# State-space scan of a hybrid trunk: the samples' token parts four-fold from memory, and like products of the second mixer side by side

## The chip, the cores and the metric

The kernel runs on one core of a Trainium2 chip. The metric is the device time of one execution in microseconds (us). A profile is one execution that the hardware profiler recorded. Its engines are TensorE (PE, with the weight loads as PEld), VectorE (DVE), ScalarE (ACT), GpSimd (POOL) and SyncE (SP), which here issues every transfer.

## The reference, cut to what matters

Four layers run over 512 prompt tokens and 8 samples of 8 tokens, 576 columns in all: convolution and attention, a feed-forward layer, a Mamba-2 mixer, and another feed-forward layer. The change is in the Mamba-2 mixer. Its scan, with 32 heads in 4 groups, head width 64 and state size 128, for each chunk of tokens:

```
acum   = cumsum(dt * a)                      # per head, within a chunk
decay  = exp(where(causal, acum_l - acum_s, -inf))
cb     = C_l . B_s                           # per group
y_diag = (cb * decay * dt) @ x               # inside the chunk
states = B . (exp(acum_end - acum) * dt) . x # what a chunk adds to the state
h      = exp(acum_end) * h + states          # from chunk to chunk
y_off  = C . h_before * exp(acum)            # what earlier chunks carry in
y      = y_diag + y_off + d_skip * x
```

The prompt is four chunks of 128 tokens and starts from zero. Each of the 8 samples is one chunk of 8 tokens and starts from a state in memory (h0). Both final states are outputs (ssm_p and ssm_s).

## The kernel before

Activations lie with channels on partitions and the 576 tokens as columns. A weight matrix comes from memory in tiles of 128 by 1024 (wr), and ACT and DVE split it into a high and a low part (wh, wl). Each projection product is three products of 128 by 288 (L160, L161, L162, tile mm). This projection stream fills TensorE nearly everywhere.

In the second mixer, `ssd(g)` is a generator that does the scan of one group, g = 0 to 3. `run(main, side)` interleaves it with units of the projection stream: the input projection of the next group, the output projection of the group before. After that a scheduler puts each engine's instructions in its own order, by estimated durations and priorities. `keep_in_program_order(m)` pins a product right behind the one written before it. Every engine works through its order strictly in turn.

Temporary tiles come from a ring of equal slots: `S(...)` takes a slot, `free(...)` returns it, and the slot returned longest ago is given out next. Whoever writes into a slot waits for its last user, and that can be a transfer to memory. TensorE's result banks are divided likewise: three for the projection (mm), two for the scan's products (aux: transposes pt, state products pst, carried products py), two for the outputs (yp), and one shared by ysp and pyo.

One scan in the order of the code, by tile names:

- btok (L951): transposes of B for the prompt. r3 (L958): B and x of the samples, each token column repeated three times; L966 and L979 transpose these, and bp, b3, xf and x3 (L968 to L985) are the parts that `finish` multiplies. b3 and x3 hold three partial terms on 96 rows, 32 rows for each. dd3 (L923 to L928) holds the factors that belong to x3.
- pc (L994), cbm: C.B, masked.
- xdt (L1007, L1009): transposes of x in five chunks of tokens, times dt; chunk 4 is the samples'.
- xde, pst, hst (L1018 to L1026): the states from chunk to chunk; out_ssm_p (L1030) writes the last one.
- es (L1035 to L1041) for the samples. `decays(r)` for each of 8 heads: acb is loaded from the kernel's own memory acd (L1047), four Relus (L1051), exponential (L1052), mask (L1053). `carried(t)`: ea loaded (L1060), exponential, py (L1064), product (L1066). `outputs(t)`: yp (L1077), and the sums into xs.
- `load` brings h0 (L1092), `begin` makes pyo and scales h0 on POOL, `finish` adds pst (L1118, b3 times x3) to h0 and writes out_ssm_s (L1120). ysp (L1145, L1150) is the samples' output.

Of the kernel before, what the change touches and what calls it, by code (L numbers as in the profile page):

```python
# [8 lines left out]
F32 = mybir.dt.float32  # L9
# [5 lines left out]
P = 128  # L15
# [25 lines left out]
for _name, _w in (  # L41
    ("ident", 128), ("m32", 32), ("prot", 128), ("blk2", 2), ("amask", 256), ("smask", 2 * 192),
    ("tri", 128), ("tris", 64), ("bmat", 64), ("bsel", 8), ("selx", 256), ("selm", 128),
    ("sel3", 192), ("bsel3", 4),
):
    CV[_name] = _n
    _n += _w
# [3 lines left out]
class Builder:  # L51
    NSLOT = 48
    EXTRA = 11
# [750 lines left out]
    def mix1(self):  # L804
# [86 lines left out]
        da = self.Z("da", W, bufs=1)  # L891
        nc.vector.scalar_tensor_tensor(da.rearrange("p (c h) -> p c h", h=32), dt.rearrange("p (c h) -> p c h", h=32), -1.0,
                                       ea.unsqueeze(1).broadcast_to([P, 5, 32]), op0=MUL, op1=MUL)
        dab = self.Z("dab", 256, rows=64, bufs=1)
# [9 lines left out]
        nc.tensor.matmul(pb[:, 160:416], self.ones[0:64, :], dab, start=True, stop=True)  # L904
        ac, de = (self.Z(n_, W, bufs=1) for n_ in ("ac", "de"))
# [16 lines left out]

        dtde, dd3 = self.Z("dtde", 32, rows=64, bufs=1), self.Z("dd3", 64, rows=96, bufs=1)  # L923
        nc.vector.tensor_tensor(dtde, dt[0:64, 128:160], de[0:64, 128:160], op=MUL)
        pe = self.ps("pe")
        for bh in range(2):
            nc.tensor.matmul(pe[0:96, bh * 32:bh * 32 + 32], self.cv("sel3", bh * 96, 96, 64), dtde, start=True, stop=True)
        nc.vector.tensor_copy(dd3, pe[0:96, 0:64])  # L928
# [15 lines left out]
        def ssd(g):  # L944
# [10 lines left out]
            r3 = []  # L955
            for a in [bf] + xs:
                r3.append(self.S("r3", 192))
                nc.scalar.activation(r3[-1].rearrange("p (b r t) -> p b r t", r=3, t=32),  # L958
                                     a[:, NP:T].rearrange("p (b t) -> p b t", t=32).unsqueeze(2).broadcast_to([P, 2, 3, 32]),
                                     AF.Copy)  # L960
            rep3 = lambda i, bh: r3[i][:, bh * 96:bh * 96 + 96]
            pt = self.ps("pt")
            b3 = []
            for bh in range(2):
                o = pt[0:96, bh * P:(bh + 1) * P]
                nc.tensor.transpose(o, rep3(0, bh), self.ident)  # L966
                bp = self.S("bp", P, F32R, rows=96)
                nc.scalar.activation(bp, o, AF.Copy)  # L968
                nc.vector.tensor_tensor(bp[64:96, :], o[64:96, :], bp[64:96, :].bitcast(F32), op=SUB)
                b3.append(self.S("b3", NP, F32R, rows=96))  # L970
                nc.vector.tensor_tensor(b3[bh].rearrange("p (b n) -> p b n", n=P),
                                        bp.bitcast(F32).unsqueeze(1).broadcast_to([96, 4, P]),
                                        self.cv("bsel3", 0, 4, 96).unsqueeze(2).broadcast_to([96, 4, P]), op=MUL)
                self.free(bp)
            x3 = []
            for bh in range(2):
                pt = self.ps("pt")
                for t in range(4):
                    nc.tensor.transpose(pt[0:96, t * P:(t + 1) * P], rep3(1 + t, bh), self.ident)  # L979
                xf = self.S("xf", NP, rows=96)  # L980
                nc.vector.tensor_tensor(hp(xf), hp(pt[0:96, :]),
                                        dd3[:, bh * 32 + 8 * g:bh * 32 + 8 * g + 8].unsqueeze(2).broadcast_to([96, 8, 64]), op=MUL)
                x3.append(self.S("x3", NP, F32R, rows=96))
                nc.scalar.activation(x3[bh], xf, AF.Copy)
                nc.vector.tensor_tensor(x3[bh][32:64, :], xf[32:64, :], x3[bh][32:64, :].bitcast(F32), op=SUB)  # L985
                self.free(xf)
                yield
            self.free(r3)
# [13 lines left out]
            xdt = []  # L1002
            for c in range(5):
                n = P if c < 4 else 64
                pt = self.ps("pt")
                for t in range(4):
                    nc.tensor.transpose(pt[0:n, t * P:(t + 1) * P], xs[t][:, c * P:c * P + n], self.ident)  # L1007
                o = self.S("xdt", NP, rows=n)
                nc.vector.tensor_tensor(hp(o), hp(pt[0:n, :]), dt[0:n, hs(c)].unsqueeze(2).broadcast_to([n, 8, 64]), op=MUL)  # L1009
                xdt.append(o)  # L1010
                if c % 2:
                    yield
            yield

            H = []
            for c in range(4):
                xde = self.S("xde", NP)
                nc.vector.tensor_tensor(hp(xde), hp(xdt[c]), de[:, hs(c)].unsqueeze(2).broadcast_to([P, 8, 64]), op=MUL)  # L1018
                pst = self.ps("pst")
                nc.tensor.matmul(pst, btok[:, c * P:(c + 1) * P], xde, start=True, stop=True)  # L1020
                hn = self.S("hst", NP)
                if c == 0:
                    nc.scalar.activation(hn, pst, AF.Copy)
                else:
                    nc.vector.tensor_tensor(hp(hn), hp(H[-1]), cd[:, hs(c)].unsqueeze(2).broadcast_to([P, 8, 64]), op=MUL)
                    nc.vector.tensor_tensor(hn, hn, pst, op=ADD)  # L1026
                self.free(xde)
                H.append(hn)
                yield
            nc.sync.dma_start(d["ssm_p"][g], H[3])  # L1030
            self.free(H.pop(), btok)
            yield

# [10 lines left out]
            def decays(r):  # L1044

                acb = self.S("acb", NP)
                nc.sync.dma_start(acb, acd[8 * g + r, 0:NP].partition_broadcast(P))  # L1047
                for c in range(4):
                    cs = slice(c * P, (c + 1) * P)
                    o = c * 32 + 8 * g + r  # L1050
                    nc.scalar.activation(acb[:, cs], acb[:, cs], AF.Relu, bias=ac[:, o:o + 1], scale=-1.0)  # L1051
                self.last_exp = nc.scalar.activation(acb, acb, AF.Exp, scale=-1.0).ins  # L1052
                nc.vector.tensor_tensor(acb, acb, cbm[:, :NP], op=MUL)  # L1053
                return acb

            def carried(t):

                ea2 = self.S("ea2", NP - P)
                for hh in range(2):
                    nc.sync.dma_start(ea2[hh * 64:hh * 64 + 64, :], acd[8 * g + 2 * t + hh, P:NP].partition_broadcast(64))  # L1060
                nc.scalar.activation(ea2, ea2, AF.Exp)
                py = self.ps("py")
                for c in range(1, 4):
                    nc.tensor.matmul(py[:, (c - 1) * P:c * P], H[c - 1][:, t * P:(t + 1) * P], cf[:, c * P:(c + 1) * P],  # L1064
                                     start=True, stop=True)
                nc.vector.tensor_tensor(ea2, ea2, py[:, 0:NP - P], op=MUL)  # L1066
                return ea2
# [44 lines left out]
            def finish(bh, behind):  # L1112

                for b4 in range(4):
                    b = 4 * bh + b4
                    pst = self.ps("pst")
                    with self.tc.issue_after(behind):
                        nc.tensor.matmul(pst, b3[bh][:, b4 * P:(b4 + 1) * P], x3[bh], start=True, stop=True)  # L1118
                    nc.vector.tensor_tensor(h0[bh][b4], h0[bh][b4], pst, op=ADD)
                    nc.sync.dma_start(d["ssm_s"][b, g], h0[bh][b4])  # L1120
                    self.free(h0[bh][b4])
                    if b4 % 2:
                        yield
# [23 lines left out]
            for t in range(4):  # L1147
                o = ysp[:, t * 64:t * 64 + 64]
                for bh in range(2):
                    nc.tensor.matmul(o, yo[bh][:, t * P:(t + 1) * P], self.cv("selm", bh * 64, 64), start=False, stop=bh == 1,  # L1150
                                     skip_group_check=True)
                nc.vector.scalar_tensor_tensor(xs[t][:, NP:], xs[t][:, NP:], self.pv("dsk", 4 * g + t), o, op0=MUL, op1=ADD)
# [34 lines left out]
        def run(main, side):  # L1187

            n, k = 30, 0
# [74 lines left out]
def constants():  # L1264
# [24 lines left out]
    for bh in range(2):  # L1289
# [6 lines left out]
        put("sel3", (tok[:, None] == bh * 32 + np.tile(np.arange(32), 3)[None, :]).astype(f), bh * 96)  # L1296
# [114 lines left out]
```

## Time and profile before

| quantity | value |
|---|---|
| three runs | 1564.84, 1567.7 and 1568.19 us; median 1567.7 |
| profiled execution | 1567.04 us; span 1565.3 |
| granted TensorE clock, mean | 0.997 |
| scan of group 0, 1, 2, 3 (us of the span) | 699.3 to 766.8, 794.3 to 868.9, 913.7 to 987.0, 1031.8 to 1098.3 |
| TensorE busy there | 63.61 of 67.50, 72.11 of 74.60, 71.13 of 73.30, 64.57 of 66.50 |

How to read the profile's rows. A row of the waits says who waited, on which tile and line, for whom: total us, times, the longest. A row of a group of instructions has line, engine, operation, tile out<-in, shape and count, then busy us, mean ns of one, and the idle time just ahead with what ended it. A row of order of time has start, duration, engine, line, operation and count. A row of the stretches has the stretch, its length, busy us of an engine (number of instructions), clock, share of the transfers, GB/s. A row of the transfers has their count, KB each, and the median us from issue to landing. TensorE's instructions overlap, so a duration is longer than the distance from one start to the next.

### The profile page before, as it was taken

What the parts mean: (1) busy time and instruction counts of PE and PEld (TensorE: products, weight loads), DVE (VectorE), ACT (ScalarE), POOL (GpSimd) and SP (SyncE); (2) the same over time, 40 slices, a digit from 0 to 9 for tenths busy, and PEclk for the clock granted to TensorE, in tenths of its full rate; (3) what the DMA queues carried; (4) which work ended last, traced back from release to release, by engine and by line L of the source; (5) the groups of instructions that cost most, each with busy time, mean ns of one, the idle gap of its engine ahead of it and who ended that gap; (6) DMA issues with size and microseconds to landing.
All of it is one profiled execution on the core that took longest, in us unless ns stands there. A gap on an engine that the chain in (4) does not pass through costs nothing. (4 is left out here: it accounts for less than half of the span.)

```text
span 1565.3 us, 28515 instructions
## 1 busy us (share of the span) xinstructions
PE 1538.9 (98%) x11661; PEld 1471.1 (94%) x11661; DVE 1002.2 (64%) x1766; ACT 642.3 (41%) x1201; POOL 148.5 (9%) x365
## 2 busy tenths in 40 slices
PE   8999999999999999999999999999999999999999
PEld 7968799999999999997998998998999999999999
DVE  7858877563564464677796677676966643563552
ACT  6247553221222222475765655656542221221220
POOL 0026101000000000011202002002010000000000
PEclk9999999999999999999999999999999999999999
DMA  8504232222222222226345235235322222222232
GB/s 235 130 30 112 86 98 88 88 82 81 81 79 85 90 87 63 76 84 183 103 131 171 93 102 182 94 107 180 99 82 81 81 83 86 88 72 92 81 86 75
DMA packets 69361, 157.61 MB, mean 101 GB/s; under 512 B 19678, under 2 KB 24030, under 8 KB 69230
## 3 DMA queue, kind: packets, MB, share of 16 engines
q1 hardware_dynamic: 69230, 155.79, 32.5%
q8 instruction: 92, 1.51, 0.4%
q14 instruction: 39, 0.32, 0.1%
HBM read 140.55 MB, written 15.21 MB: 100 GB/s over the span
## 5 line engine op out<-in xcount | busy, mean ns | idle before, releaser
L160 PE MATMUL mm<-hh,wh 128*128 128x288 f32 (+1 forms) x2288 | 682.1, 299 | 7.3 <-ACT wh L150 6.9
L162 PE MATMUL mm<-hh,wl 128*128 128x288 f32 x2288 | 681.5, 298 | 1.0 <-DVE wl L151 1.0
L161 PE MATMUL mm<-hl,wh 128*128 128x288 f32 x2288 | 678.2, 297 | 0.0
L150 ACT ACTIVATE wh<-wr 128x1024 fp32r<-128x1024 f32 (+1 forms) x215 | 223.5, 1040 | 544.6 <-issue 270.7
L160 PEld LDWEIGHTS mm<-hh,wh 128*128 128x128 f32 (+1 forms) x2288 | 431.2, 189 | 12.1 <-ACT wh L150 7.2
L162 PEld LDWEIGHTS mm<-hh,wl 128*128 128x128 f32 x2288 | 430.6, 188 | 4.8 <-issue 2.0
L161 PEld LDWEIGHTS mm<-hl,wh 128*128 128x128 f32 x2288 | 432.0, 189 | 2.6 <-DVE hl L171 0.6
L151 DVE TENSOR_TENSOR wl<-wr,wh 128x1024 fp32r<-128x1024 f32 (+1 forms) x215 | 260.1, 1210 | 82.0 <-ACT wh L150 81.9
L161 PE MATMUL mm<-yl,wh 128*128 128x288 f32 x960 | 286.1, 298 | 0.2 <-DVE yl L171 0.2
L160 PE MATMUL mm<-yh,wh 128*128 128x288 f32 x960 | 285.3, 298 | 0.7 <-DVE x L259 0.7
L162 PE MATMUL mm<-yh,wl 128*128 128x288 f32 x960 | 283.3, 296 | 0.3 <-DVE wl L151 0.3
L160 PEld LDWEIGHTS mm<-yh,wh 128*128 128x128 f32 x960 | 180.4, 188 | 4.1 <-DVE x L259 1.8
L161 PEld LDWEIGHTS mm<-yl,wh 128*128 128x128 f32 x960 | 180.8, 188 | 2.7 <-issue 1.4
L162 PEld LDWEIGHTS mm<-yh,wl 128*128 128x128 f32 x960 | 180.4, 188 | 1.5 <-issue 0.9
L259 DVE TENSOR_TENSOR x<-x,mm 128x288 f32<-128x288 f32 x192 | 84.9, 450 | 144.2 <-PE mm L162 143.8
L304 DVE TENSOR_TENSOR gbuf<-mm,rs 128x224 f32<-128x224 f32 x44 | 17.2, 391 | 107.9 <-PE mm L162 107.9
L315 ACT ACTIVATE gsilu<-gconv,par 128x512 f32<-128x512 f32 x44 | 31.8, 723 | 115.7 <-DVE gconv L312 115.7
L312 DVE SCALAR_TENSOR_TENSOR gconv<-gbuf,par,gconv 128x592 f32<-128x592 f32 x88 | 73.1, 831 | 1.5
L325 DVE TENSOR_TENSOR gsilu<-mm,gsilu 128x288 f32<-128x288 f32 x88 | 40.0, 454 | 49.6 <-PE mm L162 49.6
L830 DVE SCALAR_TENSOR_TENSOR cconv<-cbuf,par,cconv 128x600 f32<-128x600 f32 x72 | 60.2, 840 | 11.6 <-ACT cconv L828 10.7
L1051 ACT ACTIVATE acb<-acb,ac 128x128 f32<-128x128 f32 x128 | 41.3, 390 | 46.7 <-DMA acb<-acd 29.3
L307 POOL COPY fpo<-gbuf 128x2 f32<-128x2 f32 x44 | 12.4, 283 | 473.2 <-DVE gbuf L304 473.2
(311 smaller groups left out, 1600.3 us busy)
## 6 DMA issues: line engine op xcount, KB each, us to landing
wr<-in_w_gate SPq DMA_DIRECT2D x44, 512.0 KB, 3.3
wr<-in_w_up SPq DMA_DIRECT2D x44, 512.0 KB, 3.3
wr<-in_w_in_o SPq DMA_DIRECT2D x40, 512.0 KB, 3.4
wr<-in_w_down SPq DMA_DIRECT2D x32, 448.0 KB, 3.3
wr<-in_w_down SPq DMA_DIRECT2D x16, 512.0 KB, 3.5
acb<-acd SPq DMA_DIRECT2D x32, 256.0 KB, 4.1
h<-in_h SPq DMA_DIRECT2D x32, 256.0 KB, 3.6
out_ssm_s<-h SPq DMA_DIRECT2D x32, 256.0 KB, 2.5
```

What stands on the lines that cost most here:

```text
L150: nc.scalar.activation(hi[:, :n], raw[:, :n], AF.Copy)
L151: nc.vector.tensor_tensor(lo[:, :n], raw[:, :n], hi[:, :n].bitcast(F32), op=SUB)
L160: nc.tensor.matmul(out, hi[:, ws], xh[:, sl], start=i == 0, stop=False)
L161: nc.tensor.matmul(out, hi[:, ws], xl[:, sl], start=False, stop=False)
L162: nc.tensor.matmul(out, lo[:, ws], xh[:, sl], start=False, stop=i == n - 1)
L259: nc.vector.tensor_tensor(self.x[m][:, sl], self.x[m][:, sl], p[:, :HB], op=ADD)
L304: nc.vector.tensor_tensor(g[:, 290:514], p[:, 0:224], rs[:, HB:NP], op=MUL)
L312: nc.vector.scalar_tensor_tensor(cv[:, :592], g[:, k:592 + k], w(k), cv[:, :592], op0=MUL, op1=ADD)
L315: nc.scalar.activation(sl[:, :NP], cv[:, :NP], AF.Silu, bias=b)
L325: nc.vector.tensor_tensor(sl[:, HALF[half]], p[:, :HB], sl[:, HALF[half]], op=MUL)
L830: nc.vector.scalar_tensor_tensor(cv[:, :600], g[:, k:600 + k], w(k), cv[:, :600], op0=MUL, op1=ADD)
L1051: nc.scalar.activation(acb[:, cs], acb[:, cs], AF.Relu, bias=ac[:, o:o + 1], scale=-1.0)
```

## The change

It takes the r3 copies, their transposes (L966, L979) and dd3 with its products out. In their place, B of the samples is transposed once (L949 of after) and written to a new place in the kernel's own memory, bx. The samples' x parts, already transposed as xdt chunk 4, are multiplied by de (x64) and written there too (L982). `four` reads each half back with every row block four times, onto 128 rows instead of 96 (bf4, xf4, L992), and b3 and x3 are made from these, behind the states in the code. Chunk 4 of xdt now comes first.

The state products come in pairs with the two halves side by side; `finish` makes its products in pairs; transposes, py and ysp products are pinned in a row. `carried(t + 1)` is called right behind the outputs of t. The masks of a group must run in head order. Two tiles (da, dab) move into the ring, and the ring has one more slot.

```
-    EXTRA = 11
+    EXTRA = 12
...
-            r3 = []
-            for a in [bf] + xs:
-                r3.append(self.S("r3", 192))
-                nc.scalar.activation(r3[-1]..., a[:, NP:T]... repeated 3 times, AF.Copy)
...
-                nc.tensor.transpose(o, rep3(0, bh), self.ident)
...
-                    nc.tensor.transpose(pt[0:96, t * P:(t + 1) * P], rep3(1 + t, bh), self.ident)
...
+            nc.tensor.transpose(pt[0:64, 0:P], bf[:, NP:T], self.ident)
+            bx = self.dp.tile([64, NP + P], F32, name=f"bx{g}")
+            b64 = self.S("b64", P, rows=64)
+            nc.scalar.activation(b64, pt[0:64, 0:P], AF.Copy)
+            nc.sync.dma_start(bx[:, NP:], b64)
...
-            for c in range(5):
+            for c in (4, 0, 1, 2, 3):
...
-                for t in range(4):
-                    nc.tensor.transpose(pt[0:n, t * P:(t + 1) * P], xs[t][:, c * P:c * P + n], self.ident)
+                for t in (3, 0, 1, 2):
+                    m = nc.tensor.transpose(pt[0:n, t * P:(t + 1) * P], xs[t][:, c * P:c * P + n], self.ident)
+                    if t < 3:
+                        self.tc.keep_in_program_order(m)
...
+                if c == 4:
+                    x64 = self.S("x64", NP, rows=64)
+                    nc.vector.tensor_tensor(hp(x64), hp(o), de[0:64, hs(4)]..., op=MUL)
+                    nc.sync.dma_start(bx[:, 0:NP], x64)
...
+            def four(name, bh, o, n):
+                t = self.S(name, n)
+                rows = bx[bh * 32:bh * 32 + 32, o:o + n]
+                nc.sync.dma_start(t, bass.AP(tensor=rows.tensor, offset=rows.offset, ap=[[0, 4], list(rows.ap[0]), [1, n]]))
+                return t
...
+            for c0 in (0, 2):
...
+                pst = [self.ps("pst") for _ in range(2)]
+                for c in (c0 + 1, c0):
+                    m = nc.tensor.matmul(pst[c - c0], btok[:, c * P:(c + 1) * P], xde[c - c0], start=True, stop=True)
+                self.tc.keep_in_program_order(m)
...
+            b3, x3 = [], []
+            raw = [(four("bf4", bh, NP, P), four("xf4", bh, 0, NP)) for bh in range(2)]
+            yield
+            for bh, (br, xf) in enumerate(raw):
+                bp = self.S("bp", P, F32R)
+                nc.scalar.activation(bp, br, AF.Copy)
...
+                nc.scalar.activation(x3[bh], xf, AF.Copy)
...
+                if r:
+                    self.tc.add_manual_dep(m.ins, self.last_mask.name, ..., reason="masks in turn")
...
-                ea2 = carried(t)
+                if t == 0:
+                    ea2 = carried(0, False)
...
+                if t < 3:
+                    ea2 = carried(t + 1)
...
-            n, k = 30, 0
+            n, k = 29, 0
```

SyncE's queue as the third scan begins, before (h is h0; ea, acb and es are the loads of decay factors):

```order
L141 DMA wr<-in_w_in_o 128x1024 x2
L1092 DMA h_10398<-in_h 128x512
L1092 DMA h_10400<-in_h 128x512
L1092 DMA h_10402<-in_h 128x512
L1060 DMA ea_10404<-acd 64x384 x2
L1047 DMA acb<-acd 128x512
L1035 DMA es<-acd 64x8x64
L1092 DMA h_10396<-in_h 128x512
```

and after, down to the first loads of decay factors (bx is the kernel's own memory, bf and xf the four-fold reads):

```order
L141 DMA wr<-in_w_in_o 128x1024 x2
L953 DMA bx_10125<-b_10126 64x128
L992 DMA bf_10329<-bx_10125 128x1x128
L992 DMA bf_10333<-bx_10125 128x1x128
L1037 DMA es<-acd 64x8x64
L982 DMA bx_10125<-x_10146 64x512
L992 DMA xf_10331<-bx_10125 128x1x512
L992 DMA xf_10335<-bx_10125 128x1x512
L1100 DMA h_10359<-in_h 128x512
L1100 DMA h_10363<-in_h 128x512
L1100 DMA h_10361<-in_h 128x512
L1066 DMA ea_10437<-acd 64x384 x2
```

Two writes and four reads have come in, all ahead of the h0, ea and acb loads.

ACT's order at the same place, before (x is x3, hst the first state out of its result bank):

```order
L958 ACTIVATE r_10158<-xs 128x192
L984 ACTIVATE x_10180<-xf 96x512
L150 ACTIVATE wh<-wr 128x1024
L984 ACTIVATE x_10190<-xf 96x512
L1061 ACT_TABLE_LOAD
L1061 ACTIVATE ea_10404<-ea_10404 128x384
L1051 ACTIVATE acb<-acb,ac 128x128 x4
L1052 ACTIVATE acb<-acb 128x512
L1023 ACTIVATE hst<-pst 128x512
```

and after:

```order
L1025 ACTIVATE bp<-bf_10329 128x128
L1025 ACTIVATE bp<-bf_10333 128x128
L150 ACTIVATE wh<-wr 128x1024
L1032 ACTIVATE x_10342<-xf_10331 128x512
L1009 ACTIVATE hst<-pst 128x512
L1032 ACTIVATE x_10350<-xf_10335 128x512
L1067 ACT_TABLE_LOAD
```

The first x3 copy, which needs the read from bx, now stands right ahead of the state's copy (L1009), and the second right behind it; before, both x3 copies had no transfer to wait for.

DVE's order after, at the same place (b is b3, x_10342 and x_10350 are x3, x_77 and x_78 are rows of the residual):

```order
L1011 TENSOR_TENSOR hst<-hst,cd 128x512
L1033 TENSOR_TENSOR x_10342<-xf_10331,x_10342 32x512
L1012 TENSOR_TENSOR hst<-hst,pst 128x512
L259 TENSOR_TENSOR x_78<-x_78,mm 128x288
L1011 TENSOR_TENSOR hst<-hst,cd 128x512
L1028 TENSOR_TENSOR b_10348<-bp,cst 128x512
L1033 TENSOR_TENSOR x_10350<-xf_10335,x_10350 32x512
L1012 TENSOR_TENSOR hst<-hst,pst 128x512
```

The work for b3 and x3 has moved in between the steps of the states (L1011, L1012), where before there stood the multiplications for xde (L1018).

More of the change, by code (lines that the diff above doesn't have):

```diff
@@ L43 @@
     ("tri", 128), ("tris", 64), ("bmat", 64), ("bsel", 8), ("selx", 256), ("selm", 128),
-    ("sel3", 192), ("bsel3", 4),
+    ("bsel3", 4),
 ):
@@ L904, in mix1 @@
         nc.tensor.matmul(pb[:, 160:416], self.ones[0:64, :], dab, start=True, stop=True)
+        self.free(da, dab)
         ac, de = (self.Z(n_, W, bufs=1) for n_ in ("ac", "de"))
@@ L921, in mix1 @@
         nc.vector.tensor_copy(eax, pe[:, 0:64])
[L923 to L928, printed above, removed]
         acr = self.S("acr", T, rows=32)
@@ L975, in ssd @@
-            x3 = []
-            for bh in range(2):
-                pt = self.ps("pt")
-                for t in range(4):
[L979 to L987, printed above, removed]
@@ L1008, in ssd @@
                 o = self.S("xdt", NP, rows=n)
                 nc.vector.tensor_tensor(hp(o), hp(pt[0:n, :]), dt[0:n, hs(c)].unsqueeze(2).broadcast_to([n, 8, 64]), op=MUL)
-                xdt.append(o)
-                if c % 2:
+                xdt[c] = o
+                if c == 4:
+                    x64 = self.S("x64", NP, rows=64)
+                    nc.vector.tensor_tensor(hp(x64), hp(o), de[0:64, hs(4)].unsqueeze(2).broadcast_to([64, 8, 64]), op=MUL)
+                    nc.sync.dma_start(bx[:, 0:NP], x64)
+                    self.free(x64)
+                elif c % 2:
@@ L1012, in ssd @@
                     yield
             yield
-            H = []
[L1016 to L1026, printed above, removed]
+            def four(name, bh, o, n):
[3 more added lines that the diff above has]
+                return t
@@ new lines, in ssd @@
+            H = []
+            for c0 in (0, 2):
+                xde = []
+                for c in (c0, c0 + 1):
+                    xde.append(self.S("xde", NP))
+                    nc.vector.tensor_tensor(hp(xde[-1]), hp(xdt[c]), de[:, hs(c)].unsqueeze(2).broadcast_to([P, 8, 64]), op=MUL)
+                pst = [self.ps("pst") for _ in range(2)]
[3 more added lines that the diff above has]
+                yield
+                for c in (c0, c0 + 1):
+                    hn = self.S("hst", NP)
+                    if c == 0:
+                        nc.scalar.activation(hn, pst[0], AF.Copy)
+                    else:
+                        nc.vector.tensor_tensor(hp(hn), hp(H[-1]), cd[:, hs(c)].unsqueeze(2).broadcast_to([P, 8, 64]), op=MUL)
+                        nc.vector.tensor_tensor(hn, hn, pst[c - c0], op=ADD)
+                    H.append(hn)
@@ L1052, in decays, with carried @@
                 self.last_exp = nc.scalar.activation(acb, acb, AF.Exp, scale=-1.0).ins
-                nc.vector.tensor_tensor(acb, acb, cbm[:, :NP], op=MUL)
+                m = nc.vector.tensor_tensor(acb, acb, cbm[:, :NP], op=MUL)
+                if r:
+                    self.tc.add_manual_dep(m.ins, self.last_mask.name, mybir.DependencyInfo(
+                        mybir.DependencyClass.NoSync, mybir.DependencyReason.DATA), reason="masks in turn")
+                self.last_mask = m.ins
                 return acb
-            def carried(t):
+            def carried(t, close=True):
                 ea2 = self.S("ea2", NP - P)
@@ L1112, in finish @@
             def finish(bh, behind):
[L1114 to L1123, printed above, removed]
+                for b0 in (0, 2):
+                    pst = [self.ps("pst") for _ in range(2)]
+                    for b4 in (2, 3) if b0 else (1, 0):
+                        with self.tc.issue_after(behind):
+                            m = nc.tensor.matmul(pst[b4 - b0], b3[bh][:, b4 * P:(b4 + 1) * P], x3[bh], start=True, stop=True)
+                    self.tc.keep_in_program_order(m)
+                    for b4 in (b0, b0 + 1):
+                        nc.vector.tensor_tensor(h0[bh][b4], h0[bh][b4], pst[b4 - b0], op=ADD)
+                        nc.sync.dma_start(d["ssm_s"][4 * bh + b4, g], h0[bh][b4])
+                        self.free(h0[bh][b4])
+                    yield
             for t in range(4):
@@ L1149, in ssd @@
                 for bh in range(2):
-                    nc.tensor.matmul(o, yo[bh][:, t * P:(t + 1) * P], self.cv("selm", bh * 64, 64), start=False, stop=bh == 1,
-                                     skip_group_check=True)
-                nc.vector.scalar_tensor_tensor(xs[t][:, NP:], xs[t][:, NP:], self.pv("dsk", 4 * g + t), o, op0=MUL, op1=ADD)
+                    m = nc.tensor.matmul(o, yo[bh][:, t * P:(t + 1) * P], self.cv("selm", bh * 64, 64), start=False,
+                                         stop=bh == 1, skip_group_check=True)
+                    if t or bh:
+                        self.tc.keep_in_program_order(m)
+            for t in range(4):
+                nc.vector.scalar_tensor_tensor(xs[t][:, NP:], xs[t][:, NP:], self.pv("dsk", 4 * g + t),
+                                               ysp[:, t * 64:t * 64 + 64], op0=MUL, op1=ADD)
             self.free(x3, b3)
```

40 lines of the change are left out of this document (16 added, 24 removed).

## The prediction

> **What bounds the kernel now.** I read the engine totals first, then TensorE's waits in the second mixer, then the order of time around one group's scan, and the DMA issues last.
>
> ```profile
> PE 1538.9 (98%) x11661; PEld 1471.1 (94%) x11661; DVE 1002.2 (64%) x1766; ACT 642.3 (41%) x1201; POOL 148.5 (9%) x365
> ```
>
> TensorE is busy 98% of the span, so an edit pays what it takes off TensorE's stream, and costs what it makes TensorE wait. The other engines count only where a chain through them ends in a TensorE wait. Those waits in the second mixer (690 to 1112 us), by what released them; the columns are total us, times, longest:
>
> ```profile
> PE yp L1077 <- DVE acb L1053: 5.9, 4, 1.9
> PE pst L1118 <- DVE ea L1066: 2.7, 1, 2.7
> PE pt L979 <- ACT r L958: 1.1, 1, 1.1
> ...
> PE pst L1118 <- DVE h L1119: 0.4, 1, 0.4
> PE pt L979 <- DVE bp L969: 0.2, 1, 0.2
> ```
>
> These lie in the four scan stages. By place they come to 3.8, 2.4, 2.2 and 1.9 us, 10.3 in all. Summed over the four stages, the busy times agree with that:
>
> ```profile
> sum 281.90, PE 271.42 PEld 243.08 DVE 214.40 ACT 157.43 POOL 44.69; mean PE 67.85 PEld 60.77 DVE 53.60 ACT 39.36 POOL 11.17
> ```
>
> 281.90 less 271.42 is 10.5 us idle. So the change works on two accounts: TensorE work, and 10.3 us of waits that can shrink or grow.
>
> The unit of the first account is the step of the projection stream (L160 to L162), which fills TensorE between the scan's products. TensorE's order of time, start and duration:
>
> ```profile
> 921.33 0.29 PE L161 MATMUL mm<-yl,wh 128*128 128x288 f32 x1
> 921.47 0.38 PE L979 MATMUL pt<-ident,r 128*96 128x128 f32 x2
> 921.60 0.38 PE L162 MATMUL mm<-yh,wl 128*128 128x288 f32 x1
> 921.82 0.30 PE L160 MATMUL mm<-yh,wh 128*128 128x288 f32 x1
> ...
> 925.29 0.60 PE L1007 MATMUL pt<-ident,xs 128*128 128x128 f32 x4
> 925.64 0.38 PE L160 MATMUL mm<-yh,wh 128*128 128x288 f32 x1
> 925.86 0.29 PE L161 MATMUL mm<-yl,wh 128*128 128x288 f32 x1
> ...
> 936.92 0.29 PE L161 MATMUL mm<-yl,wh 128*128 128x288 f32 x1
> ...
> 941.44 0.29 PE L162 MATMUL mm<-yh,wl 128*128 128x288 f32 x1
> ```
>
> From 936.92 to 941.44 there are 34 steps, 0.133 us each. Four transposes take 925.86 − 925.29 − 0.133 = 0.44 us out of the stream, 0.11 each.
>
> **The change, TensorE's work.** The replicated transposes go: 2 at L966 and 8 at L979 in each stage. Their price is read from the four stretches between the start of L951 and that of L994, with the stream's steps counted by their weight loads:
>
> ```profile
> 699.41:708.65 9.24, 6.05 (x44) 1.00 0.39 99
> 794.36:803.83 9.47, 7.54 (x55) 1.00 0.44 132
> 913.77:922.52 8.75, 6.46 (x47) 1.00 0.38 113
> 1031.86:1040.48 8.62, 6.73 (x49) 1.00 0.30 102
> sum 36.08, PEld 26.79; mean PEld 6.70
> ```
>
> 195 steps of 0.133 are 25.9 us, L951's four transposes 4 × 0.44 = 1.8, the waits at L979 1.3. 36.1 − 25.9 − 1.8 − 1.3 leaves 7.0 us for 40 transposes. At 0.11 each they would be 4.4, and that is the other bound; I take 7.0, since the stretches hold the transposes themselves. The four small products at L927 go too: estimated 0.4, four times 0.11. One plain transpose per stage comes (L949 after): 4 × 0.11 = +0.4 to 0.5. Work: −7.0 − 0.4 + 0.5 = **−6.9 us** (−4.3 at the other bound).
>
> Pinning like products together saves changes between them and the stream. Four transposes cost 0.44, and two at L979 921.82 − 921.47 − 0.133 = 0.22, both 0.11 apiece, so a change has no price that these rows show: I put it at nothing. They are read to 0.02 or so; at that, some 40 changes saved would be −1. The products that now have 128 rows of weights where they had 96 take as many columns, and cost the same.
>
> ACT loses five copies a stage, DVE two multiplications, and gets one (x64) back. Neither engine ends the path, apart from the chain that follows.
>
> **The change, the waits.** What was a transpose now goes through memory. I follow the third stage, from the moment T at which the transposes of the sample tokens (chunk 4, which now come first) are done. Durations:
>
> ```profile
> acb<-acd SPq DMA_DIRECT2D x32, 256.0 KB, 4.1
> h<-in_h SPq DMA_DIRECT2D x32, 256.0 KB, 3.6
> out_ssm_s<-h SPq DMA_DIRECT2D x32, 256.0 KB, 2.5
> acd<-acr SPq DMA_DIRECT2D x1, 72.0 KB, 2.9
> out_ssm_p<-hst SPq DMA_DIRECT2D x4, 256.0 KB, 3.8
> cad<-cap SPq DMA_DIRECT2D x2, 271.5 KB, 6.4
> ...
> L984 ACT ACTIVATE x<-xf 96x512 fp32r<-96x512 f32 x8 | 4.7, 621 | 1.4 <-DVE xf L981 1.3
> L1023 ACT ACTIVATE hst<-pst 128x512 f32<-128x512 f32 x4 | 2.4, 596 | 4.8 <-PE pst L1020 4.7
> ...
> 935.53 0.45 DVE L259 TENSOR_TENSOR x<-x,mm 128x288 f32<-128x288 f32 x1
> 935.89 0.69 DVE L1025 TENSOR_TENSOR hst<-hst,cd 128x512 f32<-128x512 f32 x1
> 936.49 0.67 DVE L1038 TENSOR_TENSOR es<-es,ac 64x512 f32<-64x512 f32 x1
> ```
>
> On DVE one of these starts 0.6 after the other, and a residual row (L259) takes 0.4. Two multiplications like L1025 (xdt, x64), with their hand-overs, end at T+1.7. The x64 part is written to memory. Its price is not in the trace: the kernel's own writes to its memory are acd (72 KB, 2.9) and cad (271.5 KB, 6.4); 128 KB lies nearer the first, and I take 2.9, with 6.4 as the far end and 2.5 (out_ssm_s) as the near one: T+4.6. Reading it four-fold brings 256 KB, like acb: 4.1, T+8.7 (3.6 by h, 2.5 at the least).
>
> Then comes the point where it bites. ACT's order has the copy of the first x3 *ahead of* the copy of the first state out of its bank (L1009, L1023 before): 0.6 each, T+9.3 and T+9.9. DVE multiplies (0.6), adds a residual row (0.4) and adds the second state (0.6): T+11.5. That releases the bank for the second pair of state products (L1003). TensorE gets there after 55 steps (7.3), 14 transposes (1.5) and the first pair (1.7), T+10.5: a wait of 1.0 where before there was none. The pair ends at T+13.2, the third state behind more b3 and x3 work at T+14.6, the carried product (py) waits 0.3, and the last state is done at T+17.0. Here are the price of the pair, and what the last state sets off, in before (chain in order of time; SyncE's queue; ACT):
>
> ```profile
> 935.42 0.86 PE pst L1020 x2
> 936.28 0.67 PE py L1064 x6
> ...
> 941.73 1.05 PE yp L1077 x16
> ...
> 937.79 0.34 SPq L1030 DMA_DIRECT2D out_ssm_p<-hst  x1
> 941.50 0.32 SPq L1047 DMA_DIRECT2D acb<-acd  x1
> ...
> 945.66 1.28 ACT L1051 ACTIVATE acb<-acb,ac 128x128 f32<-128x128 f32 x4 [3.43 <-DMA acb<-acd]
> L1052 ACT ACTIVATE acb<-acb 128x512 f32<-128x512 f32 x32 | 19.8, 622 | 0.4
> L1053 DVE TENSOR_TENSOR acb<-acb,cbm 128x512 f32<-128x512 f32 x32 | 26.2, 821 | 20.1 <-ACT acb L1052 20.1
> ```
>
> The decay load (acb) at 941.50 starts when the state's write of 937.79 has landed, since it takes the state's slot. The order of after still has one acb load behind out_ssm_p, and now it is head 0's, behind which the other masks stand in turn. So: T+17.0, out_ssm_p 3.8, acb 4.1, four Relus 1.3, exponentials 0.6 to 1.2, masks 0.8 to 1.3: T+28.1 to 28.7. TensorE reaches the first output product (yp) at T+26.7 (13.2 at the pair's end, 0.3 waited, 85 steps 11.3, py 0.67 and pyo 1.2): a wait of 1.4 to 2.0, where before it was 1.6 there. For yp of the third token block the loads wait for slots that the first blocks give back; acb (4.1), the Relus and exponentials of both heads (3.7) and two masks (1.3) are 9.1 after the release, and TensorE has 8.25 of work (50 steps, 6.65, and 1.6 of closing and carried products): 0.85. Third stage: 1.0 + 0.3 + 1.4 + 0.85 = 3.5.
>
> The same walk with the positions of the others: first stage 3.8 (1.4 at the second pair, 1.4 at yp behind out_ssm_p and acb, 1.0 at the last yp behind out_ssm_s and acb; the wait of 2.7 before goes, because the carried factors are now prepared a block ahead); second 4.5 (1.4, 0.1, 1.8, 1.2); fourth 2.5 (0.6 at the pair, 1.9 at yp as before). Sum 14.3, against 10.3: **+4.0 us**. I take the earlier end of each span.
>
> On SyncE's queue each stage has six more transfers, 0.33 to issue, 2 us in all. The reads stand behind the write they wait for, and es, h, ea and acb behind the reads. Two weight loads stand ahead of them as cover, so the stream doesn't starve: no cost there. If that cover is gone, the projection stream itself waits, up to the 2.9 of the write.
>
> The sum is −6.9 + 4.0 = −2.9, against the profiled execution's 1567.04 (span 1565.3 and 1.7 around it): 1564.1. The median of the runs shown, 1567.7, is 0.7 above, so the forecast is **1564.8 us**.
>
> **Rivals.** *Main case, as summed*: waits grow by 1.5 to 6.5, net −0.5 to −5.5, 1562 to 1567. For it: all steps have rows near them. Chance 0.45, of which 0.20 under 1564.6 (0.2% or 3.1 us is about what can be told from no change) and 0.25 within.
>
> *The round trip is hidden.* If the four transfers in a row (write, four-fold read, out_ssm_p, acb) take out_ssm_s's 2.5 each, they are 10.0 and not 14.9: the second pair's bank is free 2.0 earlier, before T+10.5, and yp's masks are ready at about T+23.5, 2 before TensorE comes. Then only the later waits stay, about 8.3, and the time is −6.9 − 2.0, 1558.8. For it: the write's source is half of out_ssm_s's size. Against: acb itself, the same kind of read, has 4.1 as its median. Chance 0.25.
>
> The Trainium skill, "DMA: Bandwidth & Descriptors", section "Anatomy of one DMA — SWDGE (gpsimd) path", gives 2.0 us and the bytes at 436 GB/s for each transfer, on a path other than the hardware queue that carries these. By it 128 KB would take 2.3 and 256 KB 2.6, the four 10.1 (an estimate from that page), and the time this rival's 1558.8. The trace agrees with it for out_ssm_s (2.5), and not for acb (4.1), h (3.6) or out_ssm_p (3.8).
>
> *The round trip is slower, and the kernel with it.* If the write costs more than 2.9 us (cad's 6.4 is the far end), the copy ahead of the state's copy in ACT's queue comes that much later, and everything behind it: the bank, py, last state, yp. TensorE then waits about one us more in each of four stages per us of chain. From 1.5 us more per stage it is +6, 1570.8, slower; at 6.4 it is +14, 1579. For it: a memory that is written and read back at once is only in the 72 and the 271.5 KB rows, the reads share the queues with weight loads, and nothing else would start the chain earlier. Against: the size. Chance 0.30: 0.19 slower, 0.11 not far enough.
>
> **How the numbers follow.** Faster: 0.20 + 0.25 = 0.45. Same: 0.25 + 0.11 = 0.36. Slower 0.19. The range must reach into both rivals: low 1557.5 (the hidden case and a us of pinning), high 1572.5 (the write at 4.8 instead of 2.9, 4 × 1.9 = 7.6 more); one in ten lies outside on each side. The main case's own range is 1562 to 1567.
>
> **What would show it.** The stretch from btok's transposes to pc should shrink by 1.6 us a stage at equal steps. bx writes should take 2.9 and the xf reads 4.1. There should be new waits of about 1 us at the second pair of L1003, released by DVE's hst, and waits of 1 to 2 at yp L1085 released by masks; the 2.7 wait on ea should be gone. I am wrong if no wait stands at L1003 (the hidden case), if the waits there are 3 or more (the slower one), or if the projection stream itself waits for weights.

## The result: slower, and the profile after

The changed kernel takes 1592.15 us (median of 4 runs, 1590.19 to 1593.05), the kernel before 1567.32 beside it: ratio 1.0156, 95% interval 1.014 to 1.0171, or 24.8 us slower. The forecast of 1564.8 was wrong, and so was the range (1557.5 to 1572.5).

The engine totals and TensorE's longest waits of the changed kernel (total us, times, longest):

```profile
span 1589.6 us, 28485 instructions
PE 1542.8 (97%) x11621; PEld 1469.2 (92%) x11621; DVE 1002.2 (63%) x1760; ACT 634.7 (40%) x1185; POOL 159.8 (10%) x365
```

```profile
PE pst L1003 <- DVE hst L1012: 18.5, 4, 6.7
PE yp L1085 <- DVE acb L1055: 12.2, 11, 1.9
```

The span grew by 24.3 us. TensorE idles 1589.6 − 1542.8 = 46.8 us where it idled 26.4; that is 20.4 more, and 18.5 of it is one wait that the kernel before had not: once in each stage, at the second pair of state products. The waits at yp also grew, from 5.9 to 12.2, and 4.4 us of other waits of the kernel before (2.7, 1.1, 0.4 and 0.2 at pst and pt) are gone. The other 3.9 us of the span are busy time, though TensorE has 40 instructions fewer. The reason lies in the clock. Stretches around the first two of those waits (length, TensorE busy, clock, share of the transfers):

```profile
690.00:719.00 29.00, 27.13 (x197) 1.00 0.44 133
719.00:730.00 11.00, 5.93 (x14) 0.53 0.41 118
815.00:822.00 7.00, 4.31 (x25) 1.00 0.72 165
822.00:829.00 7.00, 5.66 (x14) 0.51 0.38 98
```

During each of these waits, or just behind it, the clock falls to half, and it stays there for a while. The pair itself shows it; in the third stage the first pair takes 1.88 us and the second, behind its wait, 3.37:

```profile
940.38 1.88 PE L1003 MATMUL pst<-xde,btok 128*128 128x512 f32 x4
948.90 3.37 PE L1003 MATMUL pst<-xde,btok 128*128 128x512 f32 x4 [3.44 <-DVE hst L1012]
```

Over the span the mean clock fell from 0.997 to 0.991. Part of the half clock passes while TensorE waits and costs nothing more, so its price is read from TensorE's busy time in the stretches of half clock, after and then before:

```profile
719.62:729.86 10.24, 5.79 (x13) 0.50 0.38 114
822.02:828.85 6.83, 5.51 (x13) 0.50 0.37 94
856.16:859.57 3.41, 3.41 (x25) 0.50 0.91 221
948.32:951.73 3.41, 2.83 (x5) 0.50 0.50 132
1074.61:1078.02 3.41, 3.41 (x5) 0.50 0.39 87
```

```profile
738.04:741.46 3.42, 3.42 (x16) 0.50 0.53 158
847.27:850.68 3.41, 3.41 (x17) 0.50 0.09 32
```

TensorE is busy for 20.95 us at half clock where it was for 6.83, and half of the difference, 7.1 us, is lost. Work of about −5.6 (below) and +7.1 for the clock give +1.5 of the +3.9. Of the other 2.4, about 1 lies at the program's start, where TensorE's steps shorten from 0.24 to 0.13 us at 13.0 us and in the kernel before at 11.0; the rest stays open. The wait behind which the clock falls need not be long: the two stretches of the kernel before stand behind waits of 2.73 and 1.71 us, though its wait of 1.9 us at yp has none behind it.

What the wait hangs on, in the chain of the third stage (start, us, what):

```profile
939.04 6.45 DMA xf<-bx
...
945.57 0.63 ACT x L1032
946.20 0.49 ACT hst L1009
...
947.44 0.69 DVE x L1033
...
948.15 0.70 DVE hst L1012
```

This is the chain that the prediction walked, link by link: read, x3 copy, the state's copy behind it on ACT, the state's sum on DVE, TensorE. Of the links shown only the first is far off: 6.45 us until the first half is there, not 4.1. In the first, second and fourth stage the half that the chain needs took 9.81, 6.86 and 8.48; in the first and the fourth it was the second half, whose DVE work (L1033) stands ahead of the state's sum.

Why a read of 256 KB takes that long is seen in a stretch of the fourth stage in which only these reads move. Length, TensorE busy, clock, share of the 16 transfer engines, GB/s:

```profile
1064.50:1067.40 2.90, 2.90 (x17) 1.00 0.25 90
```

A quarter of sixteen, at 90 GB/s: as much as four engines that are never idle, though the view doesn't name them. The read's source has a leading dimension of 4, the four copies (`ap=[[0, 4], ...]`).

The Trainium skill, "DMA: Bandwidth & Descriptors", section "Rules for kernel authors", says of just this that a leading zero-stride broadcast of c copies confines the whole transfer to at most c engines. The trace agrees: 0.25 of the engines for c = 4, and 0.10, which is under two sixteenths, for c = 2 (below).

### The profile page after: what moved, and what is told of

Same layout as the page of the kernel before. It is cut to its first block, busy times and chain, and to the rows that moved or that the text cites. A ratio compares the mean times of both kernels' runs of the same rounds, so it can differ in the third digit from the quotient of the medians.

```text
span 1589.6 us, 28485 instructions
## 1 busy us (share of the span) xinstructions
PE 1542.8 (97%) x11621; PEld 1469.2 (92%) x11621; DVE 1002.2 (63%) x1760; ACT 634.7 (40%) x1185; POOL 159.8 (10%) x365
## 4 chain that ended last, share of the span: by engine, by line
PE 80%; DVE 5%; DMA 5%; ACT 4%; issue 1%; SPq 0%; ACTq 0%; DVEq 0%
PE mm L162 24%; PE mm L160 24%; PE mm L161 24%; DMA xf<-bx 2%; PE mm L563 1%; ACT acb L1053 1%; PE yp L1085 1%; DMA acb<-acd 1%; DVE acb L1055 1%; PE pst L1003 1%; DVE wl L151 1%; PE py L1070 1%; ACT wh L150 1%; DVE ca L443 1%; PE pt L182 1%
## 5 line engine op out<-in xcount | busy, mean ns | idle before, releaser
L1113 POOL TENSOR_TENSOR h<-h,cds 128x512 f32<-128x512 f32 x32 | 48.1, 1531 | 158.1 <-PE pyo L1107 158.1
```

Of the source, the lines that this page charges most:

```text
L1113: nc.gpsimd.tensor_tensor(hp(h0[bh][b4]), hp(h0[bh][b4]), cds[:, b * 32 + 8 * g:b * 32 + 8 * g + 8].unsqueeze(2).broadcast_to([P, 8, 64]), ...
```

## The experiments

**The read over all engines, two ways.** Theory 1 is that the leading dimension makes the read slow, and that this makes the waits and the half clock; rival 2 that crowded queues or fresh bytes do; rival 3 that the rest of the change does. First, the copies are made by the write:

```
-                nc.sync.dma_start(t, bass.AP(tensor=rows.tensor, offset=rows.offset, ap=[[0, 4], list(rows.ap[0]), [1, n]]))
+                nc.sync.dma_start(t, bx[bh * 128:bh * 128 + 128, o:o + n])
...
+                    dst = bx[bh * 128:bh * 128 + 128, o:o + n].rearrange("(r t) n -> t r n", r=4)
+                    nc.sync.dma_start(dst, src[bh * 32:bh * 32 + 32, :].unsqueeze(1).broadcast_to([32, 4, n]))
```

> The same round trip, but the four copies are made by the write (one write per half, 32 rows outermost) and each half is read back plainly as 128 rows. In the changed kernel's trace the read's packets of 2 KB take 84 ns each and pass 24 in half a microsecond, which is four at a time, where the write's and other loads' pass about 80. Theory 1 (the read's leading dimension of four leaves it only four transfer engines, and its lateness makes the waits at L1003 and, through them, the half clock): the reads land 3 to 4 us after issue, the waits at L1003 fall from 18.5 us to under 6, the clock goes back to 0.997 or so, and the time to 1564 to 1571. Rival 2 (the read is late because the loads of h0, ea and acb share the engines, or because the bytes have just been written): reads still 6 to 10 us, time over 1585. Rival 3 (pinning, pairs and the mask order cost it): time over 1580 with the read repaired.

Measured: 1564.44 us, ratio to the kernel before 0.9981 (0.9968 to 0.9994). Second, four reads of 32 rows in place of one:

```
-                nc.sync.dma_start(t, bass.AP(..., ap=[[0, 4], list(rows.ap[0]), [1, n]]))
+                for r in range(4):
+                    nc.sync.dma_start(t[32 * r:32 * r + 32, :], bx[bh * 32:bh * 32 + 32, o:o + n])
```

> The write as it is; each four-fold read becomes four plain reads of 32 rows: eight transfers for each pair of reads instead of two. Theory 1: a pair lands about 4 us after its first issue (eight issues of 0.45 are 3.6 us of SyncE's time, so the last half lands 2 us later than with two issues); waits at L1003 5 to 10 us in all, time 1566 to 1576. Rival 2: reads still 6 to 10 us and the time over 1585. Rival 3: time over 1580.

Measured: 1560.23 us, ratio 0.996 (0.9944 to 0.9977). The transfers of the first kernel, then those of the second (KB each, median us to landing), and the second's longest waits in the mixer:

```profile
bx<-x SPq DMA_DIRECT2D x8, 256.0 KB, 3.4
xf<-bx SPq DMA_DIRECT2D x8, 256.0 KB, 2.8
```

```profile
xf<-bx SPq DMA_DIRECT2D x32, 64.0 KB, 2.0
bx<-x SPq DMA_DIRECT2D x4, 128.0 KB, 2.2
```

```profile
PE yp L1085 <- DVE acb L1055: 7.1, 7, 2.4
PE yp L1085 <- ACT acb L1053: 1.5, 2, 0.8
```

Freshly written bytes, under the same neighbours, land in 2.8 us as one plain read of 256 KB, and in 2.0 us as each of four reads of 64 KB, counted from its own issue. No wait at L1003 is left in either, and by the ratios 27 and 31 us are gone. The first kernel came out at the near end of what was expected; it still waits 13.0 us at yp, at a clock of 0.996. The second, at a clock of 0.999, is faster than expected: the 5 to 10 us of waits at L1003 did not come. Rivals 2 and 3 fall.

One thing more changed in both kernels. The scheduler put the state's copy ahead of the x3 copy in all four stages, here in the third of the second kernel:

```profile
923.65 0.60 ACT L1009 ACTIVATE hst<-pst 128x512 f32<-128x512 f32 x1 [1.96 <-PE pst L1003]
924.55 0.63 ACT L1032 ACTIVATE x<-xf 128x512 fp32r<-128x512 f32 x1 [0.30 <-DMA xf<-bx]
```

So that no wait is left at L1003 is not the quick read's doing alone. What this order is worth with a slow read, two kernels below show (two-fold reads, and the x3 copies behind the states): both stay near the changed kernel's time.

**A smaller leading dimension.** Each read split into two that are two-fold:

```
-                nc.sync.dma_start(t, bass.AP(..., ap=[[0, 4], list(rows.ap[0]), [1, n]]))
+                for r in range(0, 128, 64):
+                    nc.sync.dma_start(t[r:r + 64, :], bass.AP(..., ap=[[0, 2], list(rows.ap[0]), [1, n]]))
```

> The changed kernel, but each four-fold read is split into two reads that are two-fold (64 rows each, leading dimension 2): the same bytes and packets, twice as many transfers. Theory 1 (the leading dimension sets how many engines serve a read): packets pass two at a time, 12 in half a microsecond, so the pair of xf halves needs 128 x 84 ns = 10.8 us on its engines where it was 5.4; the banks of the second pair come about 5 us later in each stage, the waits at L1003 go from 18.5 to 35 to 42 us, with more half clock, and the time to 1610 to 1630. Rival 4 (each engine's share doesn't matter; one large read is just slow, and smaller reads are served sooner): waits at L1003 fall, 1565 to 1585. Same packets and same number of engines: 1588 to 1596.

Measured: 1596.53 us, ratio 1.0186 (1.016 to 1.0212), in two runs. The share of the engines fell as theory 1 has it, with only these reads moving:

```profile
714.00:717.00 3.00, 3.00 (x22) 1.00 0.10 38
```

Its longest waits, and the read on the chain of its first stage:

```profile
PE py L1071 <- DVE hst L1013: 25.2, 4, 10.0
PE yp L1086 <- DVE acb L1056: 11.4, 10, 1.6
```

```profile
714.03 13.12 DMA xf<-bx
```

Ten hundredths and 38 GB/s stand against 0.25 and 90, and the last of the four reads takes 13.12 us, with half the bytes of the one that took 9.81. The time is a miss: where 20 us or more were expected, its ratio can't be told from the changed kernel's 1.0156 (1.014 to 1.0171). By the time alone the number of engines could be unchanged; the share and the read speak against that. The scheduler put the state's copy ahead of the x3 copy here, so the wait moved from the second pair to py, and is 25.2 and not 35 to 42.

**The read by itself.** Four unused reads in the kernel before (da and dab moved into the ring, as in the change), each behind the landing of the one before it, ahead of the first stage's decay loads; once four-fold, once plain. The instructions stand in the same order in both.

```
+            rows = acd[0:32, 0:NP]
+            nc.sync.dma_start(dum, bass.AP(tensor=rows.tensor, offset=rows.offset, ap=[[0, 4], list(rows.ap[0]), [1, NP]]))
```

or `acd[8 * g, 0:NP].partition_broadcast(P)` as the source.

> The kernel before, with four reads of 256 KB (one for each stage, from the kernel's own memory acd, written long before) into a tile that nobody uses. Each is four-fold with the leading dimension of 4, the form of the changed kernel's reads. They go out one behind the other ahead of the first stage's decay loads, each when the one before has landed, so the distance of their issues is the price of one. Theory 1: 128 packets of 84 ns on four engines are 2.7 us, and with about 2 us around them 4.5 to 5.5 us for each, though nothing was just written and little else runs. Rival 2 (fresh bytes or crowded engines make it slow): 3 to 4 us, the same as the plain form.

> The same four unused reads of 256 KB in the same places, in the plain form that the decay loads have (one row to all 128 partitions). Theory 1: 128 packets on all engines are 0.7 us, and with about 2 us around them 2.5 to 3.5 us for each, 2 us less than the four-fold form; Rival 2: the same as the four-fold form within 0.5 us.

Measured: 1580.27 us, ratio 1.009 (1.0068 to 1.0111), and 1567.13 us, ratio 0.9999 (0.9987 to 1.0012). SyncE's queue, four-fold and then plain; the row of the two dum reads runs from the first's issue to the end of the second's:

```profile
705.83 6.08 SPq L1036 DMA_DIRECT2D dum<-acd  x2
712.01 0.42 SPq L1050 DMA_DIRECT2D acb<-acd  x1
```

```profile
699.54 3.62 SPq L1036 DMA_DIRECT2D dum<-acd  x2
703.59 0.32 SPq L1050 DMA_DIRECT2D acb<-acd  x1
```

Less the second's own issue (0.5 and 0.3), one read lasts 5.6 us and the other 3.3. During the former the share of the engines is again a quarter, with next to nothing else moving:

```profile
708.00:710.50 2.50, 0.00 (x0) 0.89 0.25 91
```

So neither fresh bytes nor crowding is needed. And reads that nobody uses cost 13 us through the loads queued behind them: each read stands in SyncE's queue until the one before it has landed, and acb is issued at 712.01 and not at 703.59. In the waits and in ACT's order of time:

```profile
PE pt L980 <- ACT r L959: 12.5, 1, 12.5
```

```profile
719.32 0.40 ACT L1054 ACTIVATE acb<-acb,ac 128x128 f32<-128x128 f32 x1 [12.47 <-DMA acb<-acd]
719.63 0.35 ACT L959 ACTIVATE r<-xs 128x192 f32<-128x192 f32 x1
```

TensorE waits for the copy r, which needs no transfer, but stands in ACT's order behind a Relu that does.

**The x3 copies behind the states.**

```
+                self.tc.add_manual_dep(m.ins, hl.name, ..., reason="states first")   # m: the x3 copy, hl: the last state
```

> The changed kernel with one more ordering: the x3 copies stand behind the last state in the scheduler's order, so that nothing of the slow read stands ahead of the states. The reads stay as slow (6 to 10 us). Theory 1: the waits at L1003 go to under 2 us and the half clock with them; the waits at yp stay (12 us), and finish may now wait for x3: 1566 to 1574. If the read hurts by other ways than its place in ACT's and DVE's order (slots held, the loads behind it), the time stays over 1580.

Measured: 1587.55 us, ratio 1.0134 (1.0117 to 1.0151), near the changed kernel. Theory 1 as I held it then missed here: it took the place in ACT's order for the only way in which the read hurts. The waits at L1003 did go, but others came. The waits, and the link of the first stage's chain that ends in the longest of them:

```profile
PE yp L1087 <- DVE acb L1057: 23.4, 11, 7.7
PE pyo L1109 <- DMA h<-in_h: 7.2, 2, 4.0
```

```profile
713.62 10.63 DMA acb<-acd
```

The acb load, issued 2.5 us behind the first xf read, needs 10.63 us, where the kernel before had 3.3 to 5.7. The share of the engines while it is under way:

```profile
714.00:721.00 7.00, 7.00 (x45) 1.00 1.01 213
722.00:724.00 2.00, 0.00 (x0) 1.00 0.26 93
```

Up to 721 the engines are full, with it and the other loads that follow the xf reads. In its last 2 us a quarter is busy, as when only a four-fold read moves, and TensorE waits. So part of the delay is crowding, and the end of it fits a load whose share stands behind the slow reads on their four engines; since no view names the engines, that is argued and not shown.

**The rest of the change by itself.** The samples' parts as before, all else as changed:

```
-            bx = self.dp.tile([64, NP + P], F32, name=f"bx{g}")
...
+            r3 = []   # and the code down to x3, as before; dd3 likewise
```

> The changed kernel with the samples' parts made as before, by three-fold copies and 40 transposes; pairs, pinning, order of the masks, carried factors a block ahead, and the extra slot stay. Theory 1: no waits at L1003 beyond 1 us, clock 0.997; the transposes cost their 6.9 us again and the other waits stay near 10: 1566 to 1572. Rival 3: the loss of 25 us stays, 1585 or more. Between, 1575 to 1582, pairs or pinning have a share of their own.

Measured: 1559.39 us, ratio 0.9957 (0.9943 to 0.9972), 7 us faster than before and faster than I expected. TensorE, here and then in the kernel with plain reads, both at a clock of 0.999:

```profile
PE 1537.7 (99%) x11661; PEld 1468.8 (94%) x11661; DVE 1003.9 (64%) x1766; ACT 638.9 (41%) x1199; POOL 158.0 (10%) x365
```

```profile
PE 1532.1 (98%) x11621; PEld 1464.6 (94%) x11621; DVE 998.3 (64%) x1760; ACT 634.2 (41%) x1183; POOL 153.1 (10%) x365
```

The round trip does save TensorE 5.6 us of work. The times can nonetheless not be told apart (1559.39 and 1560.23; the profiled spans are 1559.4 and 1557.0): with the round trip TensorE waits 9.3 us in the mixer, without it 7.1, and the rest of the 5.6 is within what the runs spread.

Three parts of that kernel were then undone one at a time: the carried factors a block ahead, the order of the masks, and the added pins.

```
-                if t == 0:
-                    ea2 = carried(0, False)
+                ea2 = carried(t, False)
```

> The kernel with the samples' parts made as before (1559.4), and in addition the carried factors asked for in their own block again and not one ahead. If that is what took out the waits of the kernel before (2.7 at pst behind ea), the time goes up by 2 to 4 us, to 1561.5 to 1563.5; if the 7 us come from elsewhere (pinning, pairs, mask order), it stays at 1558 to 1561.

> The kernel with the samples' parts made as before (1559.4), without the order of the masks. If the order brings the masks that yp needs first and so shortens the waits at yp (5.9 in the kernel before, 2.6 in this one), the time goes to 1562 to 1565; if the order costs, as the prediction had it for the first head, to 1556 to 1559.

> The kernel with the samples' parts made as before (1559.4), without any of the added pins: transposes, state products, closing products, py and ysp may be pulled apart again. The prediction put the pins at nothing, at most 1 us. Theory (pins are free of charge and of gain): 1558 to 1561. If most of this kernel's 7 us is theirs: 1564 to 1567.

Measured: 1563.41, ratio 0.9975 (0.9963 to 0.9986); 1562.59, 0.9973 (0.996 to 0.9985); 1562.16, 0.9971 (0.9959 to 0.9983). Each is still faster than the kernel before, and each gives back about 2 to 3 us by its ratio, but the intervals overlap with that of 0.9957. The first two came out where they were expected if the part matters, the third between its two cases. No single part carries the 7 us; how they divide stays open.

**Without memory.** Four copies of 32 rows from x64 and b64 straight into xf and bf:

```
-                nc.sync.dma_start(t, bass.AP(...))
+                for r in range(4):
+                    nc.sync.dma_start(t[32 * r:32 * r + 32, :], o[bh * 32:bh * 32 + 32, :])   # o: b64 or x64
```

> No round trip: xf and bf are copied straight from the tiles x64 and b64, four copies of 32 rows for each half, with no write to memory ahead. The chain loses the write and its landing (2.2 to 2.3 us). If that chain still ends some waits when the reads are quick, the time falls under that of the plain reads (1560.2), to 1556 to 1559; if the waits that are left (yp, behind the decay loads) have nothing to do with it, the same within 2 us.

Measured: 1569.25 us, ratio 1.0011 (1.0001 to 1.002), worse than both expectations. Waits for h0 loads (3.9 us at pyo) and 12 us at yp stand in its trace. The scheduler's order differs too, and I did not separate the two.

**Three plain reads and not four**, onto 96 rows:

```
-                for r in range(4):
+                for r in range(3):
```

> The changed kernel with plain reads of 32 rows (1560.2), three for each half and not four, onto 96 rows as the kernel before had them: 12 fewer issues on SyncE's queue over four stages for x and 12 for b. If SyncE's time or the place of the decay loads behind the reads still costs something, 1557 to 1559.5; if not, 1559.5 to 1561.

Measured: 1559.3 us, ratio 0.9955 (0.9938 to 0.9973): with the four plain reads and the old samples' parts, the best; the three can't be told apart. All three beat both kernels.

## Why the prediction was wrong

- *Work, −6.9*: right in kind, 5.6 measured, between its two ends (4.3 and 6.9).
- *Pins at nothing*: TensorE's busy time is 1538.6 us without and 1537.7 with them, which agrees with at most 1 us.
- *The write, 2.9*: 2.26 and 2.27 on the chain. I gave its far end the whole slow case, and it was the wrong transfer.
- *The four-fold read, 4.1*: **the step that failed.** I took acb's row, because it is a read of the same 256 KB. Its bytes are the same, its shape is not, and I named two values below 4.1 as its ends and none above. The order quoted in the text ahead shows it: the new reads stand there as 128x1x512, acb as 128x512. It measured 6.45 to 9.81 on the chain, and 5.6 by itself. The rows that I took a price from were all of transfers with 32 or 128 rows outermost.
- *The chain and its price, one us in each stage for one us*: near. Reads 2.4 to 5.7 late sum to 15.2 over four stages; the waits at the second pair are 18.5, where the walk had 1.4, 1.4, 1.0 and 0.6: 14.1 more. Of the signs that I named, the 2.7 us wait on ea is gone as said, and waits of 3.4 to 6.7 at L1003 are the sign of the slower case.
- *The masks at T+28.1 to 28.7*: a slip. The terms at their near ends add up to T+27.6, so the wait at yp in the third stage should have been 0.9 and not 1.4. It decided nothing.
- *The third rival, slower from 1.5 us more of chain*: the mechanism that happened, by its other transfer. Its far end of 1579 lacked two things: the half clock at the waits (7.1 us), and the loads held up behind the read.
- *The hidden case, 1558.8*: near what the change does when the read is quick: 1559.3 and 1560.2 with plain reads, 1564.4 with the copies in the write. That the number is so near is in part luck, since in those kernels the state's copy also stands ahead of the x3 copy.
- *The waits, +4.0 on the whole*: without the slow read they fall a little instead, from 10.3 to 9.1 us with plain reads (the 9.3 above less 0.2 at mm, which the 10.3 leaves out too). With the old samples' parts the rest of the change is worth 7 us; I had credited it with the 2.7 us of the carried factors and counted the order of the masks as a cost.

## What to carry to other kernels

A transfer's price is looked up by the shape of its access pattern, above all by its outermost dimension, and only then by its bytes; where no row has that shape, the far end of the range must be a few times the near one. Put many rows outermost (32 and 128 were quick here, 4 and 2 slow), or issue the copies one by one: here that is worth 27 to 31 us. And a new wait of TensorE can cost more than its length, because the work behind it may run at half clock: here all four waits of 3.4 us and more had this behind them, and some of 1.7 to 2.7 us too.

## What the runs showed of the hardware

- A read with a leading dimension of 4 keeps 0.25 of the transfer engines busy (90 GB/s), one with 2 keeps 0.10 (38 GB/s), and plain reads land in 2.0 us (64 KB) and in 2.8 to 3.3 us (256 KB).
- Loads that are issued behind such a read land late: one acb load took 10.63 us, the last 2 us of it at a quarter of the engines.
- In the 11 and 7 us around and behind the first two waits (6.7 and 4.0 us) the granted clock was 0.53 and 0.51, and the stretches of half clock last 3.41 us or two or three times that. The Trainium skill, "TensorE: Matmul & The Clock Gate", section "What's actually happening", has half clock after an idle window of about 3.4 us, until a busy one of that length; the trace agrees with that length, and that such waits bring it, but shorter ones brought it too: 2.73 and 1.71 us in the kernel before.
